# Compression operand stored position-first, and the reload of x2 and the last norm's weights queued after the second load of the last pass

## The chip, the cores and the metric

The kernel runs on one core of a Trainium2 chip. Its engines are TensorE (PE, with its weight loads PEld listed apart), VectorE (DVE), ScalarE (ACT), GpSimd (POOL) and SyncE (SP); SP and POOL issue the DMAs. The metric is the device time of one execution in microseconds (us), the median over repeated runs. One further execution was profiled; all rows below are from that one.

## The reference, cut to what matters

One decoder layer over 512 positions of width 1024: a norm, a combined projection, retention and a three-branch sparse attention, an output projection, and a gated MLP with a convolution, each sub-layer followed by a norm and a residual add. Two pieces matter here. The first is the compression of the keys and values of one branch into 31 overlapping blocks of 32 positions (16 apart):

```python
def compress(kv, pos_emb, w1, w2):
    n_cmp = (S - CMP_BLOCK) // CMP_STRIDE + 1          # 31 blocks, 32 wide, 16 apart
    idx = np.arange(n_cmp)[:, None] * CMP_STRIDE + np.arange(CMP_BLOCK)[None, :]
    blocks = kv[:, idx] + pos_emb[None, None, :, None, :]
    flat = blocks.transpose(0, 1, 3, 2, 4).reshape(B, n_cmp, G, CMP_BLOCK * D)
    hid = jax.nn.gelu(flat @ w1)                       # (2 heads x 31) x 2048 by 2048 x 256
    return hid @ w2
```

The second is the end of the layer: the MLP's down projection, a last norm, and the residual add.

```python
    x = x + rms_norm(mix, norm_mix_post[l])            # the kernel's "x2"
    h = rms_norm(x, norm_ffn_pre[l])
    x = x + rms_norm(conv_ffn(h, ffn_w_up[l], ffn_conv[l], ffn_w_down[l]), norm_ffn_post[l])
```

## The kernel before

Positions lie on the 128 partitions in four tiles of 128 (`t` = 0 to 3). To keep float32 accuracy, each operand of a large product is split into a rounded high half (a copy, mostly on ACT) and a low half (a subtraction, mostly on DVE), and a product is three matmuls: high by high, high by low, low by high. So a weight that has come by DMA needs an ACT copy (`wh`) and a DVE subtraction (`wl`) before TensorE can use it. `wh` and `wl` have four buffers each, handed on when the matmuls that read them are done.

The order of all instructions is fixed before the run: a planner (`_Plan`) records every operation, then places them by estimated costs, and each engine gets its own list. Since a helper at line 398 emits all of them, every row of the profile has line L398, and rows are told apart by the names of their tiles. A DMA can be given a *floor*: it may not be placed before a certain other operation. In the machine each engine, SP too, works through its list in order.

**Compression.** `post_k(t)` transposes the keys and values (`kc`) into a PSUM tile `tp`, adds the position weights on DVE into `U`, and spreads `U` into the operand `Tc` (one for keys, one for values; `TC` in the code): eight high-half copies on ACT and eight low-half subtractions on DVE for each `t`, so 32 each in all. The 128 partitions of `Tc` are 2 halves of a block by 64 dimensions. Its free dimensions are high/low `a`, head `g`, block `n` and position in the half block `j`. The product runs over the 16 positions `j`: for each, the 128 columns (a, g, n) of `Tc` are the stationary operand, and 256 columns of the high and then of the low half of the weights `w1k` or `w1v` stream past, into `cacc`:

```python
            lhs = TC[kv].rearrange("p a g n j -> p (a g n) j")[:, :, j]
            pe.matmul(a, lhs, wh[:, jj, :], start=j == 0, stop=False)
            pe.matmul(a, lhs, wl[:, jj, :], start=False, stop=j == 15)
```

That makes 64 matmuls in four blocks of 16 (8 for keys, 8 for values). The blocks alternate with the projection `w_v` (`acc`, 24 matmuls of 280 columns a block) and with transposes `tp` of the rotated queries `qn`, which POOL adds up from `ra` and `rb` of DVE. DVE's list also holds the low halves `TQ` of those queries, the value tiles `VV`, and the low halves of the next projection `w_rqk`. After the last block comes a chain for the compressed keys, from `hid` over the transpose `hT` to the first scores of the attention.

**The end.** The down projection is done by a seven-product scheme over 11 pairs of row blocks (`j` = 0 to 10) in three passes. The first pass computes four products; for each pair it forms `T` from two loads of `wdn`, one of which POOL adds in place by an accumulating DMA, and then a DVE sum of `T` with the loaded tile `raw`. The second pass computes product 4 from `t`, which ACT and DVE split from `T` after POOL has added another row block to it. The last pass computes products 2 and 3 from the row blocks loaded into `raw` (the last three pairs into `late`). Then come the last norm, with weights `wfin`, and the sum with `x2`, which was written to DRAM earlier and is read back (`x<-x_dram`). `wfin` and the four `x2` tiles are 512 KB each.

Of the kernel before, what the change touches and what calls it, by code (L numbers as in the profile page):

```python
# [10 lines left out]
F32R = mybir.dt.float32r  # L11
AF = mybir.ActivationFunctionType
ALU = mybir.AluOpType
AX = mybir.AxisListType

P = 128
NC = 32
D = 1024
# [384 lines left out]
def _body(ctx, tc, io, out, soff, coff):  # L403
# [5 lines left out]
    plan = _Plan(nc)  # L409
    pe, act, dve, pool, sync = (plan.engine(e) for e in (PE, ACT, DVE, POOL, SP))  # L410
# [5 lines left out]
    def nm(s):  # L416
        cnt[0] += 1
        return f"{s}_{cnt[0]}"
# [10 lines left out]
    def k8(shape, dt=F32, n="k"):  # L429
        return plan.tile(gp, shape, dt, nm(n), "k8", 5)  # L430
# [4 lines left out]
    def f2(shape, dt=F32, n="t"):  # L435
        return plan.tile(gp, shape, dt, nm(n), "f2", 6)
# [23 lines left out]
    def copy(o, i, scale=None, engs="A"):  # L460
        k = {} if scale is None else {"scale": scale}
        alts = {}
        if "A" in engs:
            alts[ACT] = ("activation", (o, i, AF.Copy), k)
        for c, e in (("D", DVE), ("P", POOL)):
            if c in engs and scale is None:
                alts[e] = ("tensor_copy", (o, i), {})
            elif c in engs and e == POOL:
                alts[e] = ("tensor_tensor", (o, i, scale.to_broadcast(list(o.shape))), {"op": ALU.mult})
            elif c in engs:  # L470
                alts[e] = ("tensor_scalar", (o, i, scale, None), {"op0": ALU.mult})
        plan.add(alts)

    def f(ap):
        return ap.bitcast(F32)
# [75 lines left out]
    def M(name):  # L551
        o, n = soff[name]
        return sm[:, o:o + n]
# [84 lines left out]
    def transpose4(bank, src):  # L638
        m = bank("tp").rearrange("p (a b) -> p a b", a=4)
        for q in range(4):  # L640
            transpose(m[:, q, :], src(q))
        return m
# [10 lines left out]
        dve_pool.tensor_tensor(g, g, gnw, op=ALU.mult)  # L653

    KH, KL = k8([P, 2, 2, NC + S], F32R, "KH"), k8([P, 2, 2, NC + S], F32R, "KL")
    TC = [k8([P, 2, 2, 32, 16], F32R, "Tc") for _ in range(2)]
    for kv in range(2):
        pool.memset(f(TC[kv][64:128, :, :, 31, :]), 0.0)
    pos = M("pos").rearrange("p (c a j) -> p c a j", c=2, a=2)

    kbuf, qbuf = [None] * NT, [None] * NT
# [8 lines left out]
    def post_k(t):  # L670
        ts = slice(t * P, (t + 1) * P)
        xr, kc = kbuf[t]
        kd = f2([P, 4, 2, 64], n="kd")
        rope(kd, xr, 4, t, outdup=True, eng=ROPEK)
        m = transpose4(mps, lambda q: kd[:, q, :, :].rearrange("p a d -> p (a d)"))
        kh, kl = (k.rearrange("p b g k -> p (b g) k")[:, :, NC + t * P:NC + t * P + P] for k in (KH, KL))
        copy(kh, m)
        dve.tensor_tensor(kl, m, f(kh), op=ALU.subtract)
        m = mps("tp")[:, 0:256].rearrange("p (a b) -> p a b", a=2)
        U = f2([P, 2, 2, 8, 16], n="U")  # L680
        for kv in range(2):
            transpose(m[:, kv, :], kc[:, kv * P:kv * P + P])
        for half in range(2):
            dve.tensor_tensor(U[:, half], m.rearrange("p a (n j) -> p a n j", j=16),
                              pos[:, half].unsqueeze(2).to_broadcast([P, 2, 8, 16]), op=ALU.add)
        for kv in range(2):
            for half in range(2):
                n0, u0 = 8 * t - half, 0
                if n0 < 0:
                    n0, u0 = 0, 1  # L690
                n1 = 8 * t + 8 - half
                r = slice(64 * half, 64 * half + 64)
                for g in range(2):
                    src = U[64 * g:64 * g + 64, half, kv, u0:8, :]
                    hi, lo = (TC[kv][r, a, g, n0:n1, :] for a in range(2))
                    copy(hi, src)
                    TCE.tensor_tensor(lo, src, f(hi), op=ALU.subtract)

# [35 lines left out]
    def compress_mm(kv, j4):  # L734
        if len(cbank) <= kv:
            cbank.append((mps if kv else pvps)("cacc"))
        a = cbank[kv][:, 0:256]
        wh, wl = nextw(io["w1v" if kv else "w1k"][j4], 4, 256, eng=W1E, raw=s4([P, 4, 256], n="raw"))
        for jj in range(4):
            j = 4 * j4 + jj  # L740
            lhs = TC[kv].rearrange("p a g n j -> p (a g n) j")[:, :, j]
            pe.matmul(a, lhs, wh[:, jj, :], start=j == 0, stop=False)
            pe.matmul(a, lhs, wl[:, jj, :], start=False, stop=j == 15)

# [415 lines left out]
    spills = []  # L1160
# [230 lines left out]


    TAIL = 3
    PLAIN = 1
    t2s = {}
    room = {}
# [20 lines left out]
    def wrow(j, odd):  # L1417
        return io["wdn"][2 * j + odd].rearrange("p a (b c) -> p (a b) c", b=2)

    def t_sums(j):  # L1420
        we = rawtile()
        plan.floor = sync.dma_start(we, wrow(j, 0))
        if PLAIN <= j + 1 < NP:
            t3_load(j + 1)
        plan.floor = None
        t, o = room[j]
        t2, t3 = t[:, o], t[:, o + 1]
        if j < PLAIN:
            wo = rawtile()
# [13 lines left out]
    for j in range(NP):  # L1443
# [4 lines left out]
        for n in "1567" if j < NP - 1 else "1675":  # L1448
            l, li, r, ri = jobs[n]
# [41 lines left out]
    lasts = [t_last(j) for j in range(2)]  # L1491
    for j in range(NP):
        if j + 2 < NP:
            lasts.append(t_last(j + 2))
        t = plan.tile(st, [P, 2, 512], F32R, nm("t"), ("wh", "wl")[j % 2], 4)
# [5 lines left out]
    ends = []  # L1501
    x2 = [None] * NT
    wfin = s4([P, D], n="wfin")
    plan.floor = lasts[8]
    sync.dma_start(wfin, io["bcast"][2:3, :].to_broadcast([P, D]))
    for t in (2, 3, 0, 1):
        x2[t] = (vv, av, s4, s4)[t]([P, D], n="x2")
        sync.dma_start(x2[t], io["x2"][t * P:(t + 1) * P, :]).deps[spills[t].idx] = False
    plan.floor = None
    pair = k8([P, 2, 2, 512], n="late")  # L1510
    outs = k8([P, 2, 2, 512], n="o")
    late = [pair[:, 0], pair[:, 1], s4([P, 2, 512], n="late")]
    for j in range(NP):
        wo = rawtile() if j < NP - TAIL else late[j - NP + TAIL]
        sync.dma_start(wo, wrow(j, 1))
        dve.tensor_tensor(sm_s[j][:, 1], acts[j][:, 1, 0:HT], sm_s[j][:, 1], op=ALU.subtract)
        z = wtile("z") if j < NP - TAIL else part2(s4, [P, 2, 512], "z")
        split(wo, *z)
        a12, a4 = pt([P, 2, HT], F32R, "a"), pt([P, 2, HT], F32R, "a")
        split(acts[j][:, 1, 0:HT], a12[:, 0], a12[:, 1])  # L1520
        split(sm_s[j][:, 1], a4[:, 0], a4[:, 1])
        jobs = {n: ((a[:, 0], a[:, 1]), [q[:, i] for q in z]) for n, a, i in (("2", a12, 0), ("3", a4, 1))}
        ends.append(jobs)
        if j < NP - TAIL:
            for n in "23":
                for tt in range(2):
                    product(E[n][tt], *jobs[n], tt, False, False, skip_group_check=True)
        if j == 0:
            for tt in range(2):
                norm(2 + tt, (E["4"][tt], None))  # L1530

    def end(n, tt):
        for j in range(NP - TAIL, NP):
            product(E[n][tt], *ends[j][n], tt, False, j == NP - 1, skip_group_check=True)
# [20 lines left out]
```

## Time and profile before

| | |
|---|---|
| median of 3 runs | 628.41 us (628.09 to 631.93) |
| profiled execution | 629.68 us |
| its span from first to last instruction | 627.9 us |
| around the span | 1.8 us |
| mean granted clock of TensorE | 0.995 of full |

A profile row of the timeline gives the start, the duration (of all instructions merged into it), engine, operation, output and inputs, shape and count, and in brackets how long the engine had been idle before it and what ended that idle time. Durations of neighbouring matmuls overlap, so the time that one takes from the stream is the distance between two starts.

### The profile page before, as it was taken

How to read it: one execution, taken by the hardware profiler on the slowest of the kernel's cores; microseconds unless marked ns; L12 is line 12 of the kernel's file. 1: busy time of each engine (PE TensorE's matmuls, PEld its weight loads, DVE VectorE, ACT ScalarE, POOL GpSimd, SP SyncE). 2: the span in 40 equal slices, each digit the busy share in tenths (PEclk: the TensorE clock that was granted, in tenths of full speed). 3: DMA queues.
4: the chain of work that ended last, by engine and by line, in shares of the span. 5: the costliest groups of instructions: out<-in, count | busy, mean ns of one | idle time of the engine just before them, and what ended most of it. 6: DMA issues, size and time to landing. Idle time of an engine off the chain costs nothing. (4 is left out here: it accounts for less than half of the span.)

```text
span 627.9 us, 10872 instructions
## 1 busy us (share of the span) xinstructions
PE 612.3 (98%) x3781; PEld 542.8 (86%) x3781; DVE 536.3 (85%) x1145; ACT 436.2 (69%) x898; POOL 178.6 (28%) x211
## 2 busy tenths in 40 slices
PE   8999999999999999999999999999999999999995
PEld 5888988888878888889999999999999987787874
DVE  5369876998778876589999989999999999999993
ACT  6667566778998655575867757776777767877761
POOL 0253431443124420033122332233242222321130
PEclk9999999999999999999999999999999999999998
DMA  8762448513324627448367887788868579997452
GB/s 293 275 225 86 153 130 172 134 35 92 78 67 92 144 70 264 135 165 191 84 134 188 162 197 165 187 167 198 200 156 193 127 185 228 221 252 236 160 193 85
DMA packets 42103, 102.31 MB, mean 163 GB/s; under 512 B 4800, under 2 KB 4928, under 8 KB 42048
## 3 DMA queue, kind: packets, MB, share of 16 engines
q0 software_dynamic: 18576, 41.16, 34.1%
q1 hardware_dynamic: 23328, 60.19, 27.9%
q8 instruction: 30, 0.49, 0.3%
q10 hardware_dynamic: 144, 0.26, 0.1%
q14 instruction: 25, 0.20, 0.1%
HBM read 97.40 MB, written 4.19 MB: 162 GB/s over the span
## 5 line engine op out<-in xcount | busy, mean ns | idle before, releaser
L398 DVE TENSOR_TENSOR b<-b,b 128x512 fp32r<-128x512 f32 (+1 forms) x160 | 103.9, 682 | 3.9 <-ACT b L398 2.0
L398 POOL DMA_DIRECT2D b<-wup x80 | 63.4, 936 | 153.5 <-ACT b L398 71.6
L398 ACT ACTIVATE b<-b 128x512 fp32r<-128x512 f32 (+1 forms) x160 | 92.4, 623 | 12.1 <-DMA b<-wup 4.9
L398 PE MATMUL acc<-wh,xh 128*128 128x512 f32 (+1 forms) x192 | 73.2, 386 | 1.3 <-DVE wh L398 1.3
L398 PE MATMUL acc<-wl,xh 128*128 128x512 f32 (+1 forms) x192 | 73.8, 384 | 0.0
L398 PE MATMUL acc<-wh,xl 128*128 128x512 f32 (+1 forms) x192 | 73.7, 384 | 0.0
L398 PE MATMUL X<-T,b 128*128 128x256 f32 x480 | 64.9, 284 | 0.6 <-DVE b L398 0.6
L398 PE MATMUL G<-h2h,b 128*128 128x256 f32 x320 | 64.6, 284 | 0.7 <-ACT b L398 0.7
L398 DVE TENSOR_TENSOR wl<-raw,wh 128x1024 fp32r<-128x1024 f32 (+2 forms) x48 | 56.5, 1184 | 9.4 <-ACT wh L398 9.2
L398 ACT ACTIVATE wh<-raw 128x1024 fp32r<-128x1024 f32 (+2 forms) x47 | 47.7, 1016 | 22.8 <-issue 6.9
L398 PEld LDWEIGHTS X<-T,b 128*128 128x128 f32 x480 | 60.5, 192 | 1.4 <-DVE b L398 1.0
L398 PE MATMUL X<-h2h,b 128*128 128x256 f32 x320 | 61.5, 284 | 0.2
L398 PEld LDWEIGHTS G<-h2h,b 128*128 128x128 f32 x320 | 52.9, 192 | 1.1 <-ACT b L398 1.1
L398 PEld LDWEIGHTS X<-h2h,b 128*128 128x128 f32 x320 | 51.3, 192 | 0.9 <-DVE X L398 0.5
L398 PE MATMUL G<-h2l,b 128*128 128x256 f32 x160 | 45.3, 283 | 0.0
L398 PE MATMUL X<-h2l,b 128*128 128x256 f32 x160 | 45.3, 283 | 0.0
L398 PEld LDWEIGHTS acc<-wh,xh 128*128 128x128 f32 x192 | 36.5, 192 | 7.5 <-ACT xh L398 2.2
L398 PEld LDWEIGHTS acc<-wl,xh 128*128 128x128 f32 x192 | 36.8, 192 | 5.5 <-DVE wl L398 0.3
L398 PEld LDWEIGHTS acc<-wh,xl 128*128 128x128 f32 x192 | 36.6, 191 | 5.3
L398 ACT ACTIVATE P<-P,nmx 128x256 f32<-128x256 f32 (+3 forms) x64 | 35.2, 551 | 5.5 <-DVE nmx L398 5.5
L398 PE MATMUL d<-wl,ah 128*128 128x512 f32 x88 | 34.2, 392 | 1.3 <-DVE wl L398 1.3
L398 PE MATMUL d<-wh,ah 128*128 128x512 f32 x88 | 33.1, 395 | 1.1 <-ACT wh L398 1.1
(293 smaller groups left out, 1645.5 us busy)
## 6 DMA issues: line engine op xcount, KB each, us to landing
b<-wup POOLq DMA_DIRECT2D x80, 256.0 KB, 5.5
b<-wup SPq DMA_DIRECT2D x60, 256.0 KB, 5.8
raw<-wdn SPq DMA_DIRECT2D x19, 512.0 KB, 4.8
T<-wdn POOLq DMA_DIRECT2D x21, 256.0 KB, 5.5
T<-wdn SPq DMA_DIRECT2D x10, 256.0 KB, 5.9
xraw<-xT SPq DMA_DIRECT2D x8, 256.0 KB, 5.5
xnat<-x SPq DMA_DIRECT2D x4, 512.0 KB, 6.2
raw<-w_nq SPq DMA_DIRECT2D x4, 512.0 KB, 7.2
```

What stands on the lines that cost most here:

```text
L398: i = getattr(getattr(self.nc, op.eng), method)(*a, **k)
```

## The change

The first part stores `Tc` with the position `j` outermost, so that the 128 columns for one `j` lie next to each other, and stores `U` in the matching order. The sum into `U` now reads its PSUM tile in steps of 16 elements; the spreading copies write 16 rows of 8 elements (7 for some of `t` = 0) where they wrote 128 in a row. The second part takes the loads of `wfin` and `x2` out of their place (floor: a POOL operation of the second pass) and puts them behind the load of the last pass's second pair (`FIN = 1`), with that load as the floor; the norm of the two tiles that are ready early is recorded after the second pair where it was after the first.

```diff
-    TC = [k8([P, 2, 2, 32, 16], F32R, "Tc") for _ in range(2)]
+    TC = [k8([P, 16, 2, 2, 32], F32R, "Tc") for _ in range(2)]
     for kv in range(2):
-        pool.memset(f(TC[kv][64:128, :, :, 31, :]), 0.0)
+        pool.memset(f(TC[kv][64:128, :, :, :, 31]), 0.0)
...
-        U = f2([P, 2, 2, 8, 16], n="U")
+        U = f2([P, 2, 2, 16, 8], n="U")
...
-            dve.tensor_tensor(U[:, half], m.rearrange("p a (n j) -> p a n j", j=16),
-                              pos[:, half].unsqueeze(2).to_broadcast([P, 2, 8, 16]), op=ALU.add)
+            dve.tensor_tensor(U[:, half], m.rearrange("p a (n j) -> p a j n", j=16),
+                              pos[:, half].unsqueeze(3).to_broadcast([P, 2, 16, 8]), op=ALU.add)
...
-                    src = U[64 * g:64 * g + 64, half, kv, u0:8, :]
-                    hi, lo = (TC[kv][r, a, g, n0:n1, :] for a in range(2))
+                    src = U[64 * g:64 * g + 64, half, kv, :, u0:8]
+                    hi, lo = (TC[kv][r, :, a, g, n0:n1] for a in range(2))
...
-            lhs = TC[kv].rearrange("p a g n j -> p (a g n) j")[:, :, j]
+            lhs = TC[kv][:, j].rearrange("p a g n -> p (a g n)")
...
-    plan.floor = lasts[8]
-    sync.dma_start(wfin, io["bcast"][2:3, :].to_broadcast([P, D]))
-    for t in (2, 3, 0, 1):
-        x2[t] = (vv, av, s4, s4)[t]([P, D], n="x2")
-        sync.dma_start(x2[t], io["x2"][t * P:(t + 1) * P, :]).deps[spills[t].idx] = False
-    plan.floor = None
+
+    def last_loads():
+        sync.dma_start(wfin, io["bcast"][2:3, :].to_broadcast([P, D]))
+        for t in (2, 3, 0, 1):
+            x2[t] = (vv, av, s4, s4)[t]([P, D], n="x2")
+            sync.dma_start(x2[t], io["x2"][t * P:(t + 1) * P, :]).deps[spills[t].idx] = False
+
...
-        sync.dma_start(wo, wrow(j, 1))
+        load = sync.dma_start(wo, wrow(j, 1))
+        if j == FIN:
+            plan.floor = load
+            last_loads()
+            plan.floor = None
...
-        if j == 0:
+        if j == FIN:
             for tt in range(2):
                 norm(2 + tt, (E["4"][tt], None))
```

No engine's list is reordered by the first part. On DVE, for `t` = 3 just ahead of the first `cacc` matmul, before (a row is operation, output, inputs, shape and count):

```order
 L398 TENSOR_TENSOR U_180<-tp_179,sm_67 128x256 x2
 L398 TENSOR_TENSOR KL_81<-tp_178,KH_80 128x4x128
 L398 TENSOR_TENSOR Tc_82<-U_180,Tc_82 64x128 x4
 L398 TENSOR_TENSOR Tc_83<-U_180,Tc_83 64x128 x4
 L398 TENSOR_TENSOR wl_202<-raw_200,wh_201 128x560
```

and after:

```order
 L398 TENSOR_TENSOR U_180<-tp_179,sm_67 128x256 x2
 L398 TENSOR_TENSOR KL_81<-tp_178,KH_80 128x4x128
 L398 TENSOR_TENSOR Tc_82<-U_180,Tc_82 64x16x8 x4
 L398 TENSOR_TENSOR Tc_83<-U_180,Tc_83 64x16x8 x4
 L398 TENSOR_TENSOR wl_202<-raw_200,wh_201 128x560
```

Nothing moved; only the pattern of the `Tc` writes changed. On SP, at the passage from the first to the last pass of the down projection (`raw_1218` is the first pass's last load; `raw_1261`, `raw_1268` are the last pass's first two), before:

```order
 L398 DMA raw_1218<-wdn 128x1024
 L398 DMA wfin_1253<-bcast 128x1024
 L398 DMA x_1188_1254<-x_dram 128x1024
 L398 DMA x_1189_1255<-x_dram 128x1024
 L398 DMA x_1190_1256<-x_dram 128x1024
 L398 DMA x_1191_1257<-x_dram 128x1024
 L398 DMA raw_1261<-wdn 128x1024
 L398 DMA raw_1268<-wdn 128x1024
 L398 DMA late_1258<-wdn 128x1024 x2
```

and after, where the same two loads are called `raw_1257` and `raw_1262`:

```order
 L398 DMA raw_1218<-wdn 128x1024
 L398 DMA raw_1257<-wdn 128x1024
 L398 DMA raw_1262<-wdn 128x1024
 L398 DMA wfin_1253<-bcast 128x1024
 L398 DMA x_1197_1263<-x_dram 128x1024
 L398 DMA x_1198_1264<-x_dram 128x1024
 L398 DMA x_1199_1265<-x_dram 128x1024
 L398 DMA x_1200_1266<-x_dram 128x1024
 L398 DMA late_1254<-wdn 128x1024 x2
```

The five loads moved behind two loads of `wdn`. On ACT, in the second pass (`t_1251` is the last split of that pass; `wh_1262`, now `wh_1258`, is the first weight of the last), before:

```order
 L398 ACTIVATE a_1250<-act_732 128x256
 L398 ACTIVATE t_1249<-T_1056_1122 128x512
 L398 ACTIVATE a_1252<-act_733 128x256
 L398 ACTIVATE a_1264<-act_723 128x256
 L398 ACTIVATE t_1251<-T_1056_1122 128x512
 L398 ACTIVATE wh_1262<-raw_1261 128x1024
 L398 ACTIVATE a_1265<-S_793 128x256
```

and after:

```order
 L398 ACTIVATE t_1249<-T_1056_1122 128x512
 L398 ACTIVATE a_1250<-act_732 128x256
 L398 ACTIVATE a_1252<-act_733 128x256
 L398 ACTIVATE a_1260<-act_723 128x256
 L398 ACTIVATE a_1261<-S_793 128x256
 L398 ACTIVATE t_1251<-T_1056_1122 128x512
 L398 ACTIVATE wh_1258<-raw_1257 128x1024
```

Two small splits changed places with `t_1249` and with `t_1251` and the weight copy.

## Rows read from the trace of the kernel before

**Rows 1.** The page's first part: busy time of each engine, share, instructions.

```profile
PE 612.3 (98%) x3781; PEld 542.8 (86%) x3781; DVE 536.3 (85%) x1145; ACT 436.2 (69%) x898; POOL 178.6 (28%) x211
```

**Rows 2.** The waits of PE over the span: us in total, times, longest.

```profile
PE d L398 <- DVE wl L398: 1.9, 3, 0.8
...
PE cacc L398 <- DVE Tc L398: 0.9, 1, 0.9
```

**Rows 3.** Timeline of PE, second block of compression and what follows.

```profile
67.92 0.39 PE L398 MATMUL cacc<-wl,Tc 128*128 128x256 f32 x1
...
71.05 0.38 PE L398 MATMUL cacc<-wl,Tc 128*128 128x256 f32 x1
71.27 0.29 PE L398 MATMUL acc<-wh,xh 128*128 128x280 f32 x1
```

**Rows 4.** Groups of weight loads by form, 60 to 86 us: busy, mean ns.

```profile
L398 PEld LDWEIGHTS cacc<-wl,Tc 128*128 128x128 f32 x32 | 10.1, 316 | 0.0
...
L398 PEld LDWEIGHTS acc<-wl,xh 128*128 128x128 f32 x24 | 4.8, 199 | 0.0
```

**Rows 5.** Timeline of PE in the MLP, matmuls of 256 columns.

```profile
380.14 0.28 PE L398 MATMUL G<-h2l,b 128*128 128x256 f32 x1
380.26 0.28 PE L398 MATMUL G<-h2h,b 128*128 128x256 f32 x1
```

**Rows 6.** Busy time by stretch, with granted clock (PEclk), DMA share and GB/s.

```profile
57.90:60.00 2.10, 0.79 (x6) 0.44 (x5) 1.91 (x5) 1.98 (x6) 1.17 (x2) 1.00 0.50 199
61.20:64.40 3.20, 3.20 (x15) 3.20 (x15) 3.11 (x6) 1.64 (x2) 0.44 (x1) 0.51 0.31 88
67.50:71.30 3.80, 3.80 (x21) 3.80 (x20) 3.53 (x5) 2.72 (x4) 1.05 (x2) 1.00 0.77 241
```

**Rows 7.** The waits between 57 and 99 us.

```profile
DVE TQ L398 <- ACT TQ L398: 3.6, 5, 1.5
```

**Rows 8.** Timeline of DVE, 36 to 92 us.

```profile
56.29 0.74 DVE L398 TENSOR_TENSOR U<-tp,sm 128x256 f32<-128x256 f32 x2
...
83.83 1.22 DVE L398 TENSOR_TENSOR wl<-raw,wh 128x1024 fp32r<-128x1024 f32 x1
...
91.33 0.68 DVE L398 SCALAR_TENSOR_TENSOR hid<-cu,hid 64x512 f32<-64x512 f32 x1 [0.70 <-ACT cu L398]
```

**Rows 9.** Timeline of PE, after compression: first use of `wl`, and `hT`.

```profile
86.33 0.40 PE L398 MATMUL acc<-wl,xh 128*128 128x512 f32 x1
...
93.25 0.46 PE L398 MATMUL hT<-cn,hid 64*128 64x64 f32 x4
```

**Rows 10.** The tile `Tc`: ns shortest, median, longest; first and last start.

```profile
L398 DVE TENSOR_TENSOR Tc<-U,Tc x32: 272/288/1208, 37.8 to 61.0; 64x128 fp32r<-64x128 f32 x28, 64x112 fp32r<-64x112 f32 x4
```

**Rows 11.** The chain that ended last, 540 to 628 us.

```profile
559.43 8.85 DMA T<-wdn
...
571.52 3.48 PE d L398 x14
```

**Rows 12.** Timeline, 557 to 603 us: DMA issues of SP and POOL, DVE and PE.

```profile
558.40 2.69 SPq L398 DMA_DIRECT2D x<-x_dram  x4
...
562.62 6.86 SPq L398 DMA_DIRECT2D raw<-wdn  x2
...
568.38 0.69 DVE L398 TENSOR_TENSOR T<-T,raw 128x512 f32<-128x512 f32 x1 [1.16 <-DMA T<-wdn]
...
570.27 0.49 PE L398 MATMUL d<-wh,ah 128*128 128x512 f32 x1 [0.27 <-ACT wh L398]
...
575.29 0.86 POOL L398 DMA_DIRECT2D T<-wdn  x1 [7.93 <-ACT T L398]
...
585.55 0.68 DVE L398 TENSOR_TENSOR t<-T,t 128x512 fp32r<-128x512 f32 x1
...
602.00 0.74 DVE L398 SCALAR_TENSOR_TENSOR base<-base,fs,x 128x512 f32<-128x512 f32 x1
```

**Rows 13.** DMA issues, 540 to 628 us: count, KB each, median us to landing.

```profile
T<-wdn POOLq DMA_DIRECT2D x10, 256.0 KB, 6.1
```

More of the change, by code (lines that the diff above doesn't have):

```diff
@@ L1393, in _body @@
     TAIL = 3
+    FIN = 1
     PLAIN = 1
```

## Prediction

> **What bounds the kernel now.** The page's first part comes first: TensorE is busy for 612.3 us, 98% of the span [rows 1], so the change can only help by making TensorE's own stream shorter or by closing one of its few gaps. The waits of TensorE list the gaps: all that it waited for VectorE's `wl` in the down projection is 1.9 us, and the start of compression cost 0.9 us behind `Tc` [rows 2]. A busy TensorE need not be an efficient one, so the third view is its timeline around each place that the diff touches. In the second block of compression one matmul of 256 columns starts every 0.224 us (14 steps from 67.92 to 71.05) [rows 3], while in the MLP the same 256 columns take 0.12 us [rows 5]. The clock is not the reason: it is granted at 1.00 in that block [rows 6]. Nor is it a wait, since none is listed there. What differs is the weight load: 316 ns for `Tc`, 199 ns for `xh` in the same 26 us [rows 4]. `Tc` is the only stationary operand whose columns lie 64 bytes apart, so I read the 0.224 us as the price of that stride.
>
> For the second part, the chain that ended last runs at 559.43 us into an accumulating DMA of 8.85 us for `T` [rows 11], where the median is 6.1 [rows 13]; VectorE stands idle for 1.16 us for it, and TensorE resumes only at 571.52 [rows 11, 12]. The four `x2` loads (and `wfin` just ahead of them) were issued from 558.40 on [rows 12]: 2.5 MB in flight beside it.
>
> **Part 1: compression, what TensorE gains.** With adjacent columns the step should fall from 0.224 to 0.12 us, 0.104 a matmul, 1.6 us for the 15 steps inside a block. The second, third and fourth blocks give 3 x 1.6 = 4.8 us. The first block gains little: its value half must wait for `Tc` on VectorE as before, and from 61.2 to 64.4 us the granted clock is 0.51, the 1.2 GHz level, after a stretch in which TensorE was busy for 0.79 of 2.10 us [rows 6]. At that clock 256 columns take twice 0.12, no less than now. I take 0.4 us for it, which is what the few full-speed matmuls before 61.2 save. TensorE's own sum is 5.2 us.
>
> **Part 1: what VectorE lets through.** The blocks hang on VectorE too: it makes the low halves of `w1k`, `w1v`, `w_v`, then of `w_rqk`, and the queries' `TQ`. In its list from 61 to 92 us it waits 3.6 us in all, each time for ScalarE's copy of `TQ` [rows 7], and these waits come from TensorE: ScalarE's next copy waits for a weight buffer that TensorE frees. A faster TensorE can take away these 3.6 us and no more. TensorE's margin over VectorE is small afterwards. The low half of the first `w_rqk` weight ends at 85.05 (83.83 + 1.22) and is used at 86.33, a margin of 1.28 us; `hid` ends at 92.01 and its transpose starts at 93.25, a margin of 1.24 [rows 8, 9]. So the gain at these two places is what VectorE recovers plus 1.28 or 1.24: 4.8 at most. Laying the same instructions in their order with the durations of before, each behind its engine's last one and its input, I find that VectorE recovers 2.8 of the 3.6: the value tiles `VV` still follow the last `w_v` block, and the low half of the last `w1v` weight stands behind them. That gives 2.8 + 1.28 = **4.1 us** at 86 us. What lies behind it is a list in unchanged order whose buffers and loads follow TensorE, which waits nearly nowhere until the MLP [rows 2], so the 4.1 us are kept.
>
> **Part 1: what the new pattern costs.** The 32 + 32 copies into `Tc` write runs of 8 elements, and the sum `U` reads PSUM in steps of 16. No row shows either. Below: no change, as the engines handle as many elements as before. Above, for `U`: two of them take 0.74 us, overlapped [rows 8]; 256 more elements cost VectorE 0.27 us (0.68 for 512 against 0.41 a piece here), so at half rate each gains 0.27. Six (`t` = 1 to 3) and 20 of the `Tc` subtractions stand on VectorE's list ahead of the first `cacc` matmul, which waits for the last of them [rows 2], so six slow `U` would cost 1.6 us, undiminished, since VectorE is the bound there. I take 0: the nearest row, the weight load's, is of another engine and memory; and keep 1.6 for the range. A run of 8 is no single element, so I take 0 for `Tc` as well, bounded below as a rival.
>
> The Trainium skill (Advanced Engine Details and Errata, Memory Cachelines) speaks for the one half of this and against the other: it says that SBUF wants at least two hits on a 16-byte line and that PSUM has lines of 8 bytes, two float32, with two neighbours wanted for full rate. The weight loads agree (316 ns against 199 [rows 4]). By the same page `U` would now touch a new PSUM line for each element; it names matmuls there, and no row shows VectorE doing so. By it the sum would lose the 1.6 us above.
>
> The two memsets are POOL's, in the first us, and hidden.
>
> **Part 2: the end.** The `T` that is late is the last of the first pass. Without 2.5 MB beside it, it should land after the median of 6.1, at 565.5. VectorE is then still at the list before it, until 567.22 (568.38 less the 1.16 idle), and does the sum 1.16 us earlier; ScalarE's copy, VectorE's `wl` and TensorE follow at the same distance, and TensorE resumes at 570.4 where it was 571.52 [rows 11, 12]. Bounds: 0, if the DMA is slow for other reasons than this burst; 1.6, if all that TensorE lost there goes (0.27 idle before the matmul at 570.27; the next came 1.25 later where twice 0.12 would do, 1.0 lost; and some 0.3 for the stream to fill again [rows 5, 11, 12]). I take **1.15**.
>
> The five loads do not vanish. SP's list puts them behind two `raw` loads, and the second of these waits for the buffer that VectorE's late sum frees: it was issued at 569.15 (562.62 + 6.86 less 0.33) [rows 12] and now goes near 568. So the 2.5 MB fly from 568 to some 579, at the 241 GB/s of a busy stretch [rows 6]. `x2` is first read at 602.00 [rows 12], `wfin` a little earlier: covered by some 20 us. The two `late` loads behind them on SP wait for buffers that come free later in any case. The first load of the last pass goes out no later than before. What is newly beside the burst is POOL's last accumulation, at 575.29 before, some 574.1 now [rows 12]. At the 8.85 us of the disturbed one it lands at 583.0, ScalarE needs 0.62 for its split, and VectorE's part is due at 584.4 (585.55 less 1.15): hidden, with 0.8 us to spare. ScalarE's weight copies move behind it but have idle time there. The two ACT rows that changed places cost nothing that TensorE sees.
>
> **Sum.** 4.1 + 1.15 = 5.25 us. The profiled execution took 629.68 (span 627.9 and 1.8 around it), so its like would take 624.4. It ran 1.27 above the median of the runs, 628.41, so the median should be **623.2**.
>
> **Rivals.**
> *Slow PSUM reads in `U`.* For: a stride costs the weight load 1.6 times. Against: another engine, another memory. 5.25 - 1.6 = 3.65, giving 624.8.
> *Slow `Tc` writes, the one that ends slower.* If a run of 8 is paid for like an instruction's start, the 20 subtractions on the path, 288 ns at the median [rows 10], might take twice that: 5.8 us, with `U` 7.4, so 2.1 us slower, 630.5. It decides from 0.18 us a subtraction on ((5.25 - 1.6) / 20). Against: all elements of a 32-byte run are used.
> *The burst hits the second pass.* If the last accumulation needs over 9.7 us (8.85 + 0.8), VectorE, which is full there, is late by the rest; priced at the whole second part: 624.3.
> *VectorE gives way.* If it recovers all 3.6, compression gives 4.8, and with 1.6 at the end 6.4: 622.0; with the half clock gone from the first block perhaps 621.
> *The layout does nothing*, because 0.224 is no matter of stride: 1.15 alone, 627.3. Against it: `xh` in the same stretch.
>
> The Trainium skill (TensorE: Matmul & The Clock Gate, LDWEIGHTS) gives that rival a rule: a weight load takes its columns divided by 1.2 GHz, without a term for their distance. By it `Tc` would load as fast before as after, and only the second part would count. The trace speaks against it: 316 and 199 ns for equal columns.
>
> **How the numbers follow.** Forecast 0.55; slow `U` 0.17; the burst 0.07; VectorE giving way 0.13; layout nothing 0.04; slow `Tc` 0.04. The forecast's own range is 622.3 to 624.3. The range for 8 in 10 takes in 621.2 below (half of the gain-more case) and 625.8 above (slow `U`, with some of ScalarE's copies slower too, and the burst). About 1%, 6.3 us, is what a measurement of this kernel can tell from no change; faster by more means under 622.1. That is most of the gain-more case and a little of the forecast: 0.17. Slower by over 1% would need more than the slow `Tc` case: 0.02. Within: 0.81.
>
> **What the next profile would show.** Right: weight loads of `Tc` near 199 ns, `cacc` starts 0.12 apart, `Tc` and `U` on VectorE at 0.29 and 0.41 us, the transpose `hT` near 89.2, the last `T` DMA near 6 us, no 1.16 us before its sum. Wrong: `U` near 0.7 us and a later first `cacc`; gaps of TensorE over 0.5 us between blocks behind `wl` or `qn`, perhaps with a further stretch at half clock; or a wait of ScalarE for `T` near 582.

## The result, and the profile after

The changed kernel takes 626.15 us (median of 20 runs, 623.41 to 629.08). The kernel before, run beside it, takes 631.22 (20 runs, 628.09 to 634.81). The ratio is 0.9924, with a 95% interval of 0.9906 to 0.9942: 4.8 us gained, between 3.7 and 5.9. So it is a gain clear of the noise, though smaller than the 1% (6.3 us) that the prediction held to be the least that could be told from no change. The forecast gain was 5.25 us; the forecast time, 623.2, and its range up to 625.8 were too low.

The profiled execution of the changed kernel took 629.08 us (span 627.3), the longest of its 20, so its span is no measure of the gain. It is compared stretch by stretch instead.

Page of the changed kernel, first part, which answers to [rows 1]:

```profile
PE 607.6 (97%) x3781; PEld 535.5 (85%) x3781; DVE 538.8 (86%) x1145; ACT 435.8 (69%) x898; POOL 179.7 (29%) x211
```

TensorE is busy for 4.7 us less with the same 3781 instructions. The waits of TensorE over the span (us in total, times, longest), beside [rows 2]:

```profile
PE tp L398 <- POOL qn L398: 2.1, 4, 0.7
...
PE pv L398 <- DVE pl L398: 1.5, 1, 1.5
```

The wait behind POOL's `qn` has grown to 2.1 us (before, it was 0.4). The 1.5 us behind a `pl`, VectorE's low half of a tile of the attention, is new and far from both edits. Next, compression. Two rows of TensorE's timeline in the second block, beside [rows 3]:

```profile
67.80 0.28 PE L398 MATMUL cacc<-wl,Tc 128*128 128x256 f32 x1
67.92 0.28 PE L398 MATMUL cacc<-wh,Tc 128*128 128x256 f32 x1
```

Groups of weight loads from 60 to 86 us (busy, mean ns, idle time before them), beside [rows 4]:

```profile
L398 PEld LDWEIGHTS cacc<-wl,Tc 128*128 128x128 f32 x32 | 6.1, 190 | 0.5 <-DVE wl L398 0.5
...
L398 PEld LDWEIGHTS acc<-wl,xh 128*128 128x128 f32 x29 | 5.4, 188 | 0.5 <-DVE wl L398 0.3
```

The tile `Tc` (ns shortest, median, longest), beside [rows 10]:

```profile
L398 DVE TENSOR_TENSOR Tc<-U,Tc x32: 272/288/1206, 38.6 to 61.8; 64x128 fp32r<-64x128 f32 x28, 64x112 fp32r<-64x112 f32 x4
```

A weight load of `Tc` takes 190 ns where it took 316, like any other now, and the matmuls start 0.12 us apart. The subtractions into `Tc` still take 288 ns: runs of 8 elements cost VectorE nothing. The timeline of VectorE and TensorE, 57 to 91 us, with the places that answer to [rows 8, 9]:

```profile
57.10 0.74 DVE L398 TENSOR_TENSOR U<-tp,sm 128x256 f32<-128x256 f32 x2
...
60.77 0.39 PE L398 MATMUL cacc<-wh,Tc 128*128 128x256 f32 x1 [0.94 <-DVE Tc L398]
...
73.27 0.66 PE L398 MATMUL tp<-cn,qn 128*128 128x128 f32 x4 [0.67 <-POOL qn L398]
...
82.10 1.22 DVE L398 TENSOR_TENSOR wl<-raw,wh 128x1024 fp32r<-128x1024 f32 x1
...
83.37 0.50 PE L398 MATMUL acc<-wl,xh 128*128 128x512 f32 x1
...
89.34 0.68 DVE L398 SCALAR_TENSOR_TENSOR hid<-cu,hid 64x512 f32<-64x512 f32 x1 [0.70 <-ACT cu L398]
...
90.44 0.46 PE L398 MATMUL hT<-cn,hid 64*128 64x64 f32 x4
```

The pair of `U` still takes 0.74 us, so reading PSUM in steps of 16 costs VectorE nothing. This execution reached the first `cacc` 0.79 us later than the one of before (60.77 against 59.98); 0.67 of that was there at the first transpose of the keys (36.39 against 35.72), ahead of all that was changed; distances are therefore taken from the first `cacc`. From the first `cacc` to `hT` it is 29.67 us where it was 33.27: **3.6 us gained**. VectorE's idle time behind `TQ` [rows 7] is gone; it has no gap between 62 and 88 us.

The end of the first pass: the timeline of SP, VectorE and TensorE, beside [rows 11, 12]:

```profile
557.34 11.50 SPq L398 DMA_DIRECT2D raw<-wdn  x3
...
567.76 0.69 DVE L398 TENSOR_TENSOR T<-T,raw 128x512 f32<-128x512 f32 x1
...
568.79 0.39 PE L398 MATMUL d<-wh,ah 128*128 128x512 f32 x1
...
568.93 0.45 SPq L398 DMA_DIRECT2D wfin<-bcast  x1
569.42 2.50 SPq L398 DMA_DIRECT2D x<-x_dram  x4
...
570.90 0.50 PE L398 MATMUL d<-wl,ah 128*128 128x512 f32 x1 [0.37 <-DVE wl L398]
...
574.93 0.61 PE L398 MATMUL d<-t,a 128*128 128x512 f32 x2
```

The sum of the last `T` waits for no DMA any more (1.16 us before). The accumulating DMA for it, issued at 559.91, lands after 5.3 us where it took 8.85 [rows 11] (KB each, median us to landing):

```profile
T<-wdn POOLq DMA_DIRECT2D x1, 256.0 KB, 5.3
```

The five loads go out from 568.93 on, close to the 568 of the prediction. The last 24 matmuls of the first pass take 6.14 us from 568.79 to 574.93. Before, they took 7.03, as these two rows of its timeline show:

```profile
568.48 0.39 PE L398 MATMUL d<-wh,ah 128*128 128x512 f32 x1
...
575.51 0.39 PE L398 MATMUL d<-t,a 128*128 128x512 f32 x1
```

Last, the place of the new 1.5 us. The timeline of VectorE and POOL in the changed kernel at 131 us, in the attention:

```profile
130.84 3.11 DVE L398 TENSOR_SCALAR P<-P,rr 128x384 f32<-128x384 f32 x3
...
131.39 0.88 POOL L398 DMA_DIRECT2D wl<-w_rg  x1 [4.23 <-ACT wl L398]
132.01 1.70 POOL L398 TENSOR_TENSOR rb<-xr,cn 128x256 f32<-128x256 f32 x2
```

`P` is a tile that VectorE scales in place, three times in a row here. The same three took 1.07 us before. By the tile's own row the third takes 2.45 us here. It ends 0.23 us behind POOL's two `rb` (133.94 and 133.71). The instructions on both lists are the same as before. So the 2.81 us that the changed kernel is ahead at `hT` shrink to 0.81 at the third `ct`, a transpose behind that `P` (137.94 before, 137.13 now).

### The profile page after: what moved, and what is told of

It is laid out like the page before. It is cut to its first block, busy times and chain, and to the rows that moved or that the text cites. A ratio compares the mean times of both kernels' runs of the same rounds, so it can differ in the third digit from the quotient of the medians.

```text
span 627.3 us, 10874 instructions
## 1 busy us (share of the span) xinstructions
PE 607.6 (97%) x3781; PEld 535.5 (85%) x3781; DVE 538.8 (86%) x1145; ACT 435.8 (69%) x898; POOL 179.7 (29%) x211
## 5 line engine op out<-in xcount | busy, mean ns | idle before, releaser
L398 POOL DMA_DIRECT2D T<-wdn x21 | 18.2, 876 | 56.0 <-ACT T L398 46.5
```

Source lines behind the costliest of these rows:

```text
L398: i = getattr(getattr(self.nc, op.eng), method)(*a, **k)
```

## The experiments

Theory A is the prediction's mechanism: a shorter weight load, as far as VectorE lets it through, and an end without its stall, with the two gains adding up, and only the base of the forecast too low. Its rivals are named in each expectation. Since executions of one program differ by several us, three measures were read from every trace: the distance from the first `cacc` to `hT`, the last 24 matmuls of the first pass, and the duration of that third `P`.

| run | ratio to before (95%) | first `cacc` to `hT` | last 24 | third `P` |
|---|---|---|---|---|
| before (first trace) | | 33.27 | 7.03 | 0.42 |
| changed (first trace) | 0.9924 (0.9906 to 0.9942) | 29.67 | 6.14 | 2.45 |
| e0_before | 0.9991 (0.9965 to 1.0016) | 33.05 | 7.00 | 0.42 |
| e0_after | 0.9916 (0.9886 to 0.9947) | 29.67 | 6.15 | 2.45 |
| e1_layout | 0.9927 (0.9893 to 0.9960) | 29.61 | 7.25 | 0.42 |
| e2_loads | 0.9968 (0.9938 to 0.9998) | 33.64 | 5.53 | 0.42 |
| e4_qn_dve | 0.9902 (0.9875 to 0.9930) | 30.53 | 5.44 | 2.44 |
| e5_hold | 0.9909 (0.9881 to 0.9937) | 29.64 | 6.06 | 0.42 |
| e3_stride | one run | 30.67 | 5.69 | 0.42 |
| e6_fin0 | one run | 29.65 | 5.83 | 0.42 |
| e7_before_more | one run | 32.64 | 9.17 | 0.42 |
| e7_after_more | one run | 31.96 | 5.65 | 0.41 |
| e8_best | 0.9919 (0.9891 to 0.9946) | 29.66 | 5.99 | 0.42 |
| e9_after | 0.9910 (0.9876 to 0.9943) | 29.66 | 5.44 | 0.41 |

**The base: the kernel before against itself.** No edit.

> The kernel before, unchanged, against itself. Its median should be near 631, as in the 20 runs beside the changed kernel (631.22), and not near the 628.41 of the first three runs; the ratio should lie within 0.3 percent of 1. Theory A (the prediction's mechanism, with its base taken too low): near 631. Rival: the base was right and the later runs of before were slow by chance, then near 628.4. Its second trace also shows which stretches differ between two executions of the same program: the start of the projections (first transpose at 35.7 us in the first trace) and the sum P at 133.6 us.

Median 632.85, and 632.82 for the 32 runs beside it, the lowest of which is 629.46. Two of the first three runs (628.09 and 628.41) lie below all of these 32. So 628.41 was low for this kernel. The three are the first of the 20 runs beside the changed kernel, and the four shortest of those 20 (628.09 to 628.63) are all among the first six; whether chance made them short, or something that the first runs had in common, stays open.

**The changed kernel again.** No edit.

> The changed kernel again. Theory A: ratio 0.992 as before, and its trace shows the compression's gain of some 3.5 us still there at the end of the attention. Rival B: VectorE's sum P beside POOL's work near 131 us costs 2 us in every execution of the changed kernel (3.11 us for three instructions where 1.07 stood before), because the work now stands 2.8 us earlier against a DMA issue; then P takes about 3.1 us there again, and the markers behind it (ct near 137) gain only about 1.5 us net of the start.

The gain holds, and so does the 29.67. `P` took 2.45 us again, which at this point spoke for rival B.

**Each part alone.** First all the diff's lines on `TC` and `U`, on the kernel before, of which these stand for the rest:

```diff
-    TC = [k8([P, 2, 2, 32, 16], F32R, "Tc") for _ in range(2)]
+    TC = [k8([P, 16, 2, 2, 32], F32R, "Tc") for _ in range(2)]
...
-        U = f2([P, 2, 2, 8, 16], n="U")
+        U = f2([P, 2, 2, 16, 8], n="U")
```

> The kernel before with the new layout of Tc and U alone; the reloads stay in their old place. Theory A: 4.1 us of the gain, ratio 0.9935, weight loads of Tc near 188 ns, and the 1.16 us of VectorE behind the last T of the first pass still there. Rival C (the whole gain is the layout's, the moved loads give nothing, as the changed kernel's trace with only 0.4 us gained there suggests): ratio 0.992, as of both. Rival D (the layout gives little, the end gives most): ratio above 0.997.

Then only the lines on `last_loads` and `FIN`:

```diff
-    plan.floor = lasts[8]
...
+        if j == FIN:
+            plan.floor = load
+            last_loads()
+            plan.floor = None
```

> The kernel before with the moved loads alone; Tc as before. Theory A: 1.15 us, ratio 0.998, the last T of the first pass lands after some 6 us, no idle time of VectorE before its sum. Rival C: ratio 1.000, since other waits of VectorE (for raw, for ScalarE) take the place of that one. Rival D: ratio below 0.995.

The layout alone gives 0.9927 and the whole of the compression's gain, with the old end (7.25). The loads alone give 0.9968, the old compression and the new end (5.53). The two gains, 4.6 and 2.0 us of 632.8, make 6.6, where both together give 5.3; the intervals are wide enough for 3.6 + 1.5 as well. The times alone do not part theory A from rival C of e1_layout (0.9927 against 0.992); rivals C and D fall on the traces: of these two stretches, each part changes its own and not the other.

**Which step of the columns costs.** The edit of the changed kernel (`kv` is 0 for keys, 1 for values):

```diff
-    TC = [k8([P, 16, 2, 2, 32], F32R, "Tc") for _ in range(2)]
+    TC = [k8([P, 8, 2, 2, 32, 2], F32R, "Tc"), k8([P, 4, 2, 2, 32, 4], F32R, "Tc")]
...
-            lhs = TC[kv][:, j].rearrange("p a g n -> p (a g n)")
+            lhs = TC[kv][:, j // (2 * kv + 2), :, :, :, j % (2 * kv + 2)].rearrange("p a g n -> p (a g n)")
```

> The changed kernel with the 128 columns of Tc for one position 2 elements (8 bytes) apart for the keys and 4 elements (16 bytes) apart for the values, instead of adjacent. Theory A1: the weight load pays for each further 16-byte piece that it touches; then 8 bytes apart load as fast as adjacent ones (188 ns), or a little slower, and 16 bytes apart about as slowly as 64 bytes did (316). Theory A2: any step other than 1 costs the full price: 316 for both. Rival: the load time is not a matter of the step but of the tile's place or of the writes: 188 for both. The sum P near 131 us is looked at here too: 2.45 us if the changed program always has it.

TensorE's timeline across the border from keys to values, which lies at 71.69 us:

```profile
71.09 0.28 PE L398 MATMUL cacc<-wl,Tc 128*128 128x256 f32 x1
71.21 0.28 PE L398 MATMUL cacc<-wh,Tc 128*128 128x256 f32 x1
...
71.92 0.40 PE L398 MATMUL cacc<-wl,Tc 128*128 128x256 f32 x1
72.15 0.40 PE L398 MATMUL cacc<-wh,Tc 128*128 128x256 f32 x1
```

The weight loads from 70.6 to 71.5 us, among the keys:

```profile
L398 PEld LDWEIGHTS cacc<-wh,Tc 128*128 128x128 f32 x4 | 0.8, 196 | 0.0
```

And from 72.0 to 73.3 us, among the values:

```profile
L398 PEld LDWEIGHTS cacc<-wl,Tc 128*128 128x128 f32 x4 | 1.3, 330 | 0.0
```

Columns 8 bytes apart load in 196 ns and step by 0.12 us; 16 bytes apart they load in 330 ns and step by 0.23, as at 64 bytes. Theory A1 is what this trace shows: the price is one of the step, it is paid at 16 bytes and not at 8, and it is no higher at 64. The Trainium skill (Advanced Engine Details and Errata, Memory Cachelines) asks for at least two hits on each 16-byte line of SBUF; two columns 8 bytes apart can share such a line and two columns 16 bytes apart cannot, and the trace agrees.

**POOL's `qn`.** Where the changed kernel's order has one of the four sums `qn` on POOL, it is issued on VectorE:

```diff
             for op in self.schedule():
+                if op.eng == POOL and any(t.startswith("qn_") for t in op.tiles) and DVE in op.alts:
+                    op.eng = DVE
```

> The changed kernel with the four sums qn on VectorE, at the place in the order where POOL had them; nothing else moves. Theory A: what held back the layout's gain (3.6 us at the transpose hT where 4.1 was forecast, with 2.1 us of TensorE's waits now for POOL's qn of 2.1 us each) is POOL; with qn on VectorE at some 0.6 us each those waits shrink, and the distance from the first cacc to hT falls from 29.67 to 28.5 or less. Rival B: VectorE was as full, and four more sums of 0.6 us on it push the low halves wl back: the distance stays at 29.7 or grows by up to 2.4, and the waits turn into waits for wl.

The distance grows to 30.53, and the waits of TensorE from 57 to 99 us become

```profile
PE tp L400 <- DVE qn L400: 2.8, 4, 1.1
```

A faster `qn` (0.69 us each where POOL took 2.10) does not help, since it stands in VectorE's list. Rival B, with a size of 0.9 us of its 2.4. The whole execution is no slower for it (0.9902, an interval that overlaps those of the changed kernel).

**Is VectorE the bound?** Two idle sums at one place of VectorE's list, in the changed kernel and in the one before:

```diff
+                if op.eng == DVE and any(t.startswith("wl_169") for t in op.tiles) and not self.held:
+                    for _ in range(2):
+                        self.nc.vector.tensor_tensor(self.idle, self.fill, self.fill, op=ALU.add)
+                    self.held = True
```

> The changed kernel with two idle sums of 512 elements on VectorE (0.68 us each, 1.3 together) ahead of the low half of the third weight block of compression, near 77 us, behind the last operand of POOL's fourth qn. They compute nothing that is used. Theory A (VectorE, full without a gap from 62 to 88 us, is what now sets the time of hT): the distance from the first cacc to hT grows by the whole 1.3, from 29.65 to 30.95. Rival (POOL's qn or TensorE itself sets it, VectorE has slack): it grows by at most 0.5.

> The same two idle sums at the same place of the kernel before, where VectorE idles for 1.49 us behind that low half, waiting for ScalarE's copy of TQ. Theory A (before, TensorE set the time there and VectorE had room): the distance from the first cacc to hT stays near the 33.0 to 33.6 of the three traces, and the 1.49 us of idle time shrink to 0.2. Rival (VectorE was the bound there already): it grows by 1.3, to 34.4 or more.

The two sums took 2.38 us in both, more than the 1.3 that I had expected: the first took 0.68, the second, which stands beside POOL's `qn`, 1.66. VectorE's timeline in the changed kernel with the sums:

```profile
79.57 2.38 DVE L400 TENSOR_TENSOR idle<-cn 128x512 f32<-128x512 f32 x2
```

And in the kernel before with the sums:

```profile
79.79 2.38 DVE L400 TENSOR_TENSOR idle<-cn 128x512 f32<-128x512 f32 x2
```

In the changed kernel `hT` comes 2.30 us later (31.96 for 29.66): nearly all of the 2.38 is paid. Before, it comes no later at all (32.64). That trace had the full clock in compression, which the three others of the old `Tc` had not (below), so the fair measure starts behind that stretch, at the third block of `w_v`. In the kernel before it starts at

```profile
78.42 0.29 PE L398 MATMUL acc<-wh,xh 128*128 128x280 f32 x1
```

and with the sums, up to `hT`, at

```profile
80.77 0.29 PE L402 MATMUL acc<-wh,xh 128*128 128x280 f32 x1
...
95.63 0.46 PE L402 MATMUL hT<-cn,hid 64*128 64x64 f32 x4
```

That is 14.86 us with the sums and 14.83 without (`hT` at 93.25). So VectorE's idle time and margin took in sums of that size before, and now there is no room for them. The rival falls in both.

**The third `P`.** One idle instruction on POOL ahead of the two `rb`:

```diff
+                if op.eng == POOL and any(t.startswith("rb_537") for t in op.tiles) and not self.held:
+                    self.nc.gpsimd.memset(self.idle, 0.0)
+                    self.held = True
```

> The changed kernel with one idle POOL memset of 64 elements ahead of the two sums rb that start 0.52 us behind the third P of VectorE near 131 us. Theory A: those sums and P compete for something that VectorE and POOL share; in the two traces of the changed kernel rb starts 0.52 us behind P's start and P takes 2.45 us, in the four of the other kernels 0.555 us behind and P takes 0.42. With rb some 0.15 us later P should take 0.42 again, the distance from the second to the third ct should fall from 17.8 to 15.8, and the time by 2.0 us against the changed kernel (ratio to before near 0.989). Rival B: the 2.45 us come from something else in the changed program; then P stays at 2.45, or the memset itself collides.

The tile `P` there, from 132.4 to 134.5 us (ns shortest, median, longest):

```profile
L401 DVE TENSOR_SCALAR P<-P,rr x3: 416/416/417, 132.5 to 133.2; 128x384 f32<-128x384 f32 x3
```

`P` takes 0.42 us. But it does so without the memset too, in e1, e3, e6, e7_after_more and e9; among the eight traces with the new layout and no memset it is long in three. So not every execution of the changed program has the long `P`, and rival B of the run e0_after falls. That the memset removes it is not shown by two traces. In all fourteen, `P` is long where the first `rb` starts 0.52 us behind it, and short where it starts 0.55 us or more behind it. The border of 105 ns that the run e9_after names, for POOL's DMA issue ahead of `P`, does not hold: in e7_after_more the issue starts 107 ns ahead and `P` takes 0.41 us. What the two compete for, and what sets the 0.03 us between the two cases, stays open.

**The loads one place earlier, and a version with both.** On the changed kernel, then on the kernel with the memset:

```diff
-    FIN = 1
+    FIN = 0
```

> The changed kernel with FIN = 0: the five loads behind the first instead of the second load of the last pass. Theory A: the two gaps of TensorE at the last pair of the first pass (0.27 and 0.76 us, or up to 0.47 and 0.76, in all three traces with the old place; 0 or 0.37 with the new) come from the 2.5 MB that fly beside the last accumulating DMA of the first pass. Behind the first load the burst begins once the first raw buffer is free, earlier than behind the second, so part of it may come back: gaps of 0.4 to 1.0. Rival: the order matters only against the first pass's own loads, which both places respect: gaps as with FIN = 1, at most 0.4. The third P near 131 us: 2.45 if the changed program always has it.

> The changed kernel with the idle POOL memset ahead of rb and with the five loads behind the first load of the last pass (FIN = 0). Theory A: P at 0.42 us, the last 24 matmuls of the first pass in at most 6.15 us, no new wait; the 2.0 us of the collision, in three of the nine traces without that memset, are worth 0.7 us on average: ratio to before near 0.990, and no difference from the changed kernel that can be measured in so many runs. Rival: the loads one place earlier delay the last pass, then its ratio is above that of the changed kernel.

And the changed kernel a third time, with no edit.

> The changed kernel once more, beside the version before it on the same chip: ratio near 0.992 if the two earlier results (0.9924 and 0.9916) hold. Theory A for its trace: distance from the first cacc to hT 29.65, clock at full from 57 to 75 us, the third P at 0.42 or 2.45 us by whether POOL's issue of the DMA starts less or more than 105 ns ahead of it.

With `FIN = 0` the last 24 matmuls take 5.83 and 5.99 us, no worse than with `FIN = 1` (5.44 to 6.15 in eight traces). Both places lie behind the last load of the first pass, and between these two the runs show no difference. The version with both is at 0.9919, the changed kernel beside it at 0.9910: no difference that was measured, and no version here beats the changed kernel.

## Why the prediction was wrong in its time, and right in its gain

**The step that failed is the last of the sum**: "It ran 1.27 above the median of the runs, 628.41, so the median should be 623.2." The gain was taken from the median of three runs as if that were the kernel's time. Those three spread over 3.8 us; the 20 runs that they begin have a median of 631.22, and 32, 11 and 14 runs beside the experiments have 632.82, 632.33 and 631.29. From 631.22, the forecast's own 5.25 gives 625.97; measured were 626.15. That this lies between the times of two rivals, 624.8 for a slow `U` and 627.3 for a layout that does nothing, comes from the base alone; neither happened. The range held the bounds of the costs, but nothing for the base, though the spread of the three was in front of me and nearly as large as the whole gain. That the gain came out so close is luck in part: one of its two terms was too high and the other too low, and the first was near for another reason than the one given, as the next paragraphs show.

**Weight load and step: right.** 190 ns and 0.12 us, as forecast; the rival "the layout does nothing" is out by run e1.

**"4.1 us at 86 us": the bound was right, the size 0.35 too high there, and VectorE's part near by luck.** From the first `cacc` to the first use of the low half of `w_rqk` it is now 22.60 us where it was 26.35: 3.75. The margin there is used up: the low half ends at 83.32 and is used at 83.37. VectorE recovered 2.52 us on the way there, where the prediction took 2.8 of 3.6, since it would still wait for `VV` behind the last `w_v` block. That wait did not come; all 3.6 us of its idle time are gone. But about 0.9 us of them went into longer sums, which a reckoning "with the durations of before" could not see, most of it at one place. Without its waits, VectorE makes two low halves beside a sum of POOL where it had made them just behind it. Before:

```profile
72.61 0.73 POOL L398 TENSOR_TENSOR rb<-xr,cn 128x256 f32<-128x256 f32 x1
...
73.34 1.88 DVE L398 TENSOR_TENSOR wl<-raw,wh 128x1024 fp32r<-128x1024 f32 x2
```

And in the changed kernel:

```profile
72.83 2.66 DVE L398 TENSOR_TENSOR wl<-raw,wh 128x1024 fp32r<-128x1024 f32 x2
...
73.17 1.72 POOL L398 TENSOR_TENSOR rb<-xr,cn 128x256 f32<-128x256 f32 x1
```

In e4_qn_dve POOL is idle there, and the same two take 1.87 us again:

```profile
73.91 1.87 DVE L400 TENSOR_TENSOR wl<-raw,wh 128x1024 fp32r<-128x1024 f32 x2
```

So POOL bears on the bound after all, through VectorE's durations. At `hT` the margin of 1.24 was counted in full, but 0.42 of it remains (`hid` ends at 90.02, `hT` starts at 90.44): `hT` follows its neighbour in TensorE's list without a wait, and what comes late is the low half of `w_rqk`, 30 matmuls ahead. So 3.6 there instead of 4.0. The waits that the prediction listed under "wrong", TensorE behind `qn`, did come (2.1 us), as what VectorE's full list looks like from TensorE.

**The half clock of the first block: the premise did not hold.** Busy time by stretch in compression (us, then PE, PEld, DVE, ACT and POOL; granted clock, DMA share, GB/s), in the kernel before:

```profile
57.00:75.00 18.00, 16.69 (x101) 16.23 (x101) 15.90 (x25) 10.37 (x19) 8.65 (x6) 0.91 0.41 133
```

The same stretch of the changed kernel, and its start-up:

```profile
6.00:16.00 10.00, 8.81 (x31) 6.82 (x32) 9.09 (x13) 7.82 (x11) 0.00 (x0) 0.83 0.99 353
57.00:75.00 18.00, 15.22 (x117) 14.13 (x116) 17.36 (x27) 12.09 (x21) 10.37 (x7) 1.00 0.41 133
```

And of the kernel before with the two idle sums:

```profile
6.00:16.00 10.00, 7.49 (x20) 5.68 (x21) 8.72 (x13) 7.28 (x11) 0.00 (x0) 0.66 0.89 322
57.00:75.00 18.00, 16.70 (x107) 16.15 (x106) 16.68 (x25) 12.24 (x22) 10.49 (x8) 1.00 0.40 131
```

For the first microseconds the profile has no granted clock (its records of it begin at 10.05 us in the kernel before), and there the matmuls tell more. One of 512 columns takes 0.42 us of the stream up to that point and 0.24 behind it:

```profile
9.19 0.63 PE L398 MATMUL acc<-wl,xh 128*128 128x512 f32 x1
9.61 0.60 PE L398 MATMUL acc<-wh,xl 128*128 128x512 f32 x1
10.04 0.41 PE L398 MATMUL acc<-wl,xh 128*128 128x512 f32 x1
10.28 0.39 PE L398 MATMUL acc<-wh,xl 128*128 128x512 f32 x1
```

So the start-up begins at the pace of 1.2 GHz, and so it is in all fourteen traces. In five of them the clock rises once, between 5.9 and 13.6 us, and stays up until compression: three with the old `Tc`, which all drop to 1.2 GHz between 0.8 and 2.3 us behind the first `cacc`, and two with the new one (e3_stride, e6_fin0), which do not. In the nine others it rises by 5.3 us, falls again between 7.4 and 8.7, and is up once more by 15.4; none of these drops in compression, not even the one with the old `Tc` (e7_before_more). So the new layout (in e3_stride with its wider steps) came through compression at the full clock in both traces that had no drop before it, and the old one in none of three; what kept the clock up in the ninth, old one stays open.

With the clock at full the old compression took 32.64 us to `hT`, where the other three took 33.05 to 33.64, and behind the stretch in question they are alike (14.83 to 14.88). So 0.6 of the first pair's 3.6 us is what the half clock had cost the kernel before, and against the full clock the layout gained 3.0. The forecast counted on the half clock in both kernels.

**Slow reads of PSUM, slow writes of `Tc`: neither came.** 0.74 and 288 ns, to the last digit what they were. The rule that PSUM wants two neighbours in a line of 8 bytes (the Trainium skill, Advanced Engine Details and Errata, Memory Cachelines) does not show on VectorE here.

**"I take 1.15" at the end: right, a little low.** The two gaps of TensorE are gone or down to 0.37, and the last 24 matmuls take a median of 5.67 us in the eight traces with `FIN = 1` against 7.14 in the four with the old place: 1.5, inside the bounds of 0 and 1.6. In the first pair of traces it was 0.9. (The 9.17 of e7_before_more holds 3.4 us at half clock, from 574.88 on; without it the old place has 7.03, and the gain is 1.4.) The accumulating DMA for the last `T` took 8.25 to 9.17 us in the four traces with the old place and 4.16 to 5.26 in the ten with the new ones. The burst does not hit the second pass: from its start to the last `d` it is 45.66 us (574.93 to 620.59), before 45.68.

**What no step had** is the long `P`: 2.0 us in three of eight traces, 0.75 on average if these are typical; no timed run shows this share, as the versions with the memset are no faster (0.9909 and 0.9919). 3.6 + 1.5 less 0.75 is 4.35, and without it 5.1; timed were 4.8, with 3.7 to 5.9.

## What to carry to other kernels

Lay the stationary operand out so that neighbouring columns share 16 bytes: a busy TensorE hides a weight load that takes 1.7 times as long, and the distance of two starts shows it. What a faster TensorE brings is what the next engine's idle time and margins allow. The list of that engine gives a bound, but with the durations of before it misses what the engine pays once its idle time is gone and its sums stand beside those of a third one: 0.9 of 3.6 us here. And where a gain is smaller than the spread of the runs, the forecast is a difference: the base needs a range of its own.

## What the runs showed of the hardware that was not expected

A step of 16 bytes between the columns of a weight costs as much as one of 64 (330 and 316 ns for 128 columns), one of 8 bytes next to nothing (196 against 190). The 16 and 8 bytes are from one trace. VectorE reads PSUM in steps of 64 bytes at full speed (0.74 us for two of 256 elements, either way).

A `P` on VectorE that started 0.52 us ahead of two POOL sums `rb` took 2.45 us instead of 0.42 and ended 0.23 us behind the second of them; with 0.55 us between the starts it took 0.42. Beside POOL's sums two low halves on VectorE took 2.66 us instead of 1.88, and an idle sum 1.66 instead of 0.68. The Trainium skill (SBUF — State Buffer, SBUF: two separate sides) tells of a port pair that VectorE and GpSimd take in turn, for whole instructions. The row of `P` agrees with a lock, though here the one that started first by the profile was the one that waited.

Executions of one program differ by 8 us (629.46 to 637.87 in 32). In the traces the difference is in two places. The first transpose of the keys starts between 35.47 and 38.79 us: of the 2.23 us between two traces of the changed kernel (36.39 and 38.62), 1.02 are there when the first low half of a weight is used (8.12 and 9.14), and the rest comes behind it, where the one has 3.4 us at half clock (from 8.57 on) and the other 6.8 (from 8.36 on). The first pass takes 63 to 68 us: where it took 67.99 (e0_before), ScalarE waited 6.7 us for the DMAs of `T` and VectorE 4.2 for those of `raw`, and where it took 63.06 (e4_qn_dve), 1.2 and 0.6.
